# Row maxima of the attention as four narrow matmuls through the identity, and sixteen modulation units moved from GpSimd to VectorE

## The chip, the cores and the metric

The kernel runs on one core of a Trainium2 chip. The metric is the device time of one execution in microseconds; lower is better. The core has TensorE (PE in the profile; PEld is its weight load), VectorE (DVE), ScalarE (ACT), GpSimd (POOL) and SyncE (SP), which here issues the loads.

## The reference

A two-layer trunk over 512 latent tokens and 256 context tokens, width 1024. Layer 0 mixes with dense grouped attention (16 heads on 4 key heads, head size 64), layer 1 with a Conformer convolution, and each layer ends with a squared-ReLU MLP of width 4096. The parts that the change touches:

```python
def modulate(x, g, shift, scale):
    return rms_norm(x, g) * (1 + scale) + shift

# (shift, scale, gate) of both sub-layers: linear(SiLU(c)), 6 vectors of 1024 a layer
# x += gate * f(modulate(x, g, shift, scale))

def gqa_attend(q, k, v):
    p = jax.nn.softmax(gqa_scores(q, k), axis=-1)
    return jnp.einsum('bhgqk,bkhd->bqhgd', p.astype(v.dtype), v)
```

For latent tokens the keys are all 768 tokens.

## The kernel before

Activations stand transposed, features on the 128 partitions and tokens along the free axis. The products are split in high and low fp32r parts and take three passes (`passes`, L630 to L632).

**Modulation units.** Ten of the twelve vectors are computed as the program goes, in 80 units: a unit is a 128x1024 f32 tile `mraw` of the modulation weight, multiplied with the SiLU row `sbc` and summed along the free axis to one column of `mcol`. `mod_run(k)` runs the next k units; `mod_fetch` keeps two tiles loaded (tag `mraw`, two buffers), and a load is issued on SyncE when the unit before the last is done with its buffer. 64 units run on VectorE, one instruction each (L664) with its sum read out (DVE_READ_ACCUMULATOR). The first 16, those of two vectors that the output projection and the MLP need, run inside the attention loop on GpSimd: a product (L657), five halvings (L660) and a last addition (L662) into a buffer `mparts`, which VectorE reduces after the loop, before `mod_final` adds the bias.

**The attention loop.** It runs over 99 groups g; head h and key tile t are `divmod(g, 6)`. It stands in `manual_schedule` for TensorE, ScalarE and VectorE, so that these engines take their work in the order of the program. A group issues, in this order: the scores of tile t (two matmuls 128x512, L1420 and L1421) and their exponential on ScalarE; for tile 3 the split of it into high and low parts (`phl`, L1432, on VectorE); the product with v of tile g - 2 (L1439; for tile 3 the three passes); a piece of the row maxima of the next head but one or so; q's copies for later heads (L1365 and L1367); the steps of `finish` for every second head (`dn`, `rd`, `ou`, `hl`, L1469 to L1479); and at t = 2 the modulation units, two in heads 0, 4 and 8, one in each other up to head 12.

**Row maxima.** For a head, `row_max` has for each of four query tiles two matmuls 128x384 into a PSUM bank `sn` (L1377), each followed by a maximum on VectorE (L1379). `max_diag` takes the negative maximum over the pieces, with queries on the partitions (`nn`, 128x4, L1383), and multiplies it with the identity into four diagonal matrices side by side (L1385, 128x512). `max_row`, two groups later, multiplies a matrix of ones with these (L1392, 512 columns), which gives a bank with the row of 512 maxima in every partition, and ScalarE copies one partition into row 64 of `q2`, so that the second scores matmul subtracts the maximum. Three banks hold `sn`, three `mm`, two `pv`. The first two heads' maxima are made ahead of the loop, in the q projection.

Names in the rows are those of the tiles: `t` is any tile that `tmp()` gives, and the numbers behind names are of the tile's instance.

Of the kernel before, what the change touches and what calls it, by code (L numbers as in the profile page):

```python
# [344 lines left out]
def trunk(ctx: ExitStack, tc: tile.TileContext, par, cst, xT, cT, modp, modt, wqkv, wo, up, down, pw1, wtoe, pw2, out):  # L345
    nc = tc.nc
    pers = ctx.enter_context(tc.tile_pool(name="pers", bufs=1))
    wraw = ctx.enter_context(tc.tile_pool(name="wraw", bufs=2))
    whl = ctx.enter_context(tc.tile_pool(name="whl", bufs=4))
    sm = ctx.enter_context(tc.tile_pool(name="sm", bufs=4))  # L350
    tp = ctx.enter_context(tc.tile_pool(name="tp", bufs=1))

    def tmp(n=512, dt=F32):
        return tp.tile([P, n], dt, tag="t", name="t", bufs=6)
# [25 lines left out]
    ident = cst_t[:, 0:P]  # L380
    sel = pcol("sel", 0, 2)[0:4]

    ones = pers.tile([P, P], F32, name="ones")
    nc.vector.memset(ones, 1.0)
    inv_d = pers.tile([P, P], F32, name="inv_d")
    nc.vector.memset(inv_d, 1.0 / D)
    ones_r = pers.tile([P, P], F32R, name="ones_r")
    nc.scalar.copy(ones_r, ones)

    def act_set(name):  # L390
        tc.keep_in_program_order(nc.scalar.preload_act_table_set(name))
# [210 lines left out]
    fin = [None]  # L602
# [31 lines left out]
    mcol = pers.tile([P, 12, NT], F32, name="mcol")  # L634
# [3 lines left out]
    sbc = pers.tile([P, D], F32, name="sbc")  # L638

    def mod_slot(l, v):  # L640
        return l * 6 + v

    mod_raw = []
# [5 lines left out]
            nc.sync.dma_start(raw, modt[idx, b, :, i * 1024:(i + 1) * 1024])  # L649
            mod_raw.append(raw)  # L650

    def mod_unit(raw, idx, b, i, pool):
        l, v = MODV[idx]
        s = mod_slot(l, v)
        if pool is not None:
            n = 1024
            nc.gpsimd.tensor_tensor(out=raw, in0=raw, in1=sbc, op=ALU.mult)  # L657
            while n > 32:
                n //= 2
                nc.gpsimd.tensor_tensor(out=raw[:, :n], in0=raw[:, :n], in1=raw[:, n:2 * n], op=ALU.add)  # L660
            o = idx * 128 + (2 * b + i) * 16
            nc.gpsimd.tensor_tensor(out=pool[:, o:o + 16], in0=raw[:, :16], in1=raw[:, 16:32], op=ALU.add)  # L662
            return
        nc.vector.scalar_tensor_tensor(  # L664
            out=tmp(1024, mybir.dt.bfloat16), in0=raw, scalar=1.0, in1=sbc, op0=ALU.mult, op1=ALU.mult,
            accum_out=mcol[:, s, 2 * b + i:2 * b + i + 1])
        if b == 3 and i == 1:
            mod_final(l, v)

    def mod_final(l, v):  # L670
        s = mod_slot(l, v)
        mb = pcol("modb", l * 48 + v * 8, 8)
        nc.vector.tensor_tensor(out=mcol[:, s], in0=mcol[:, s], in1=mb, op=ALU.add)
        if v in (1, 4):
# [254 lines left out]
    with ExitStack() as st0:  # L929
# [83 lines left out]
        tiles, rows, w_hl, tots, msq, lrow, l_r, srow = {}, {}, {}, {}, {}, {}, {}, {}  # L1013
# [227 lines left out]
        for t_, gname in ((tk, "kg"), (tq, "qg")):  # L1241
            go = COFF[gname][0]
            for ci, cn in enumerate(("cos", "sin")):
                co = COFF[cn][0]
                for hf in range(2):
                    with tc.issue_after(tiles["pool"].ins):
                        nc.gpsimd.tensor_tensor(
                            out=t_[:, :, ci, hf * 32:(hf + 1) * 32],
                            in0=cst_t[:, co:co + 128].rearrange("p (t d) -> p t d", t=4),
                            in1=cst_t[:, go + hf * 32:go + (hf + 1) * 32].unsqueeze(1).to_broadcast([P, 4, 32]),  # L1250
                            op=ALU.mult)
        kg = cst_t[:, COFF["kg"][0]:COFF["kg"][0] + HD]

        def vview(t):
            return t.rearrange("p t (a b d) -> p t a b d", a=2, b=3)
# [123 lines left out]
                nc.vector.tensor_reduce(out=nmx[h][:, tt, b:b + 1], in_=sn[:, :384], op=ALU.max, axis=AX.X)  # L1379

        def max_diag(h):
            nm = sm.tile([P, 4], F32, tag="nn", name="nn")
            nc.vector.tensor_reduce(out=nm, in_=nmx.pop(h), op=ALU.max, axis=AX.X, negate=True)  # L1383
            dg = tmp(512, F32R)
            nc.vector.tensor_tensor(  # L1385
                out=dg.rearrange("p (t q) -> p t q", t=4), in0=ident.unsqueeze(1).to_broadcast([P, 4, P]),
                in1=nm.unsqueeze(2).to_broadcast([P, 4, P]), op=ALU.mult)
            return dg

        def max_row(h, dg):  # L1390
            mb = ms_bank()
            nc.tensor.matmul(mb, lhsT=ones_r, rhs=dg, start=True, stop=True)  # L1392
            nc.scalar.copy(qs[h][1][HD:HD + 1], mb[HD:HD + 1])

        for c in range(2):
# [89 lines left out]
        mparts = tmp(384)  # L1485
        pend = {}
        pvs = {}
        with tc.manual_schedule(engines={mybir.EngineType.PE, mybir.EngineType.Activation, mybir.EngineType.DVE}):
            for g in range(NH * NKT + 3):
                h, t = divmod(g, NKT)  # L1490
# [22 lines left out]
                while tasks.get(g):  # L1513
                    tasks[g].pop(0)()
                if t == 2 and h < NH:
                    with tc.issue_after(last_scale.ins):
                        mod_run(2 if h % 4 == 0 and h < 12 else 1 if h < 13 else 0, mparts)
                if g == NH * NKT - 12:
                    w_prefetch(1)
        with tc.issue_after(fin[0].ins):  # L1520
            for i in range(2):
                l, v = MODV[i]
                nc.vector.tensor_reduce(out=mcol[:, mod_slot(l, v)],
                                        in_=mparts[:, i * 128:(i + 1) * 128].rearrange("p (n q) -> p n q", q=16),
                                        op=ALU.add, axis=AX.X)
                mod_final(l, v)

    def proj_residual(l, v, after):
        sq = SqAcc(nc.vector)
# [298 lines left out]
```

## Time and profile before

| | |
|---|---|
| three runs | 1312.84, 1311.84, 1305.18 us (median 1311.84) |
| the profiled execution | 1310.47 us, its span 1308.7 us |
| mean granted TensorE clock | 0.977 |
| busy share | TensorE 94%, VectorE 76%, ScalarE 53%, GpSimd 19% |
| GpSimd busy | 247.1 us, of which 105.37 us from 156.27 to 285.25 us |

The attention loop begins at 147.0 us with head 0; head 1 begins at 156.27, head 12 at 285.25, head 13 at 295.18 and head 14 at 304.79. The start of a head is here the start of its first scores matmul on TensorE. The span is what the profiler recorded; the execution's own time lies 1.8 us above it.

### The profile page before, as it was taken

Reading aid. Unit: us, or ns where it says so; the run is one execution under the profiler, and the core shown is the slowest. Engines: PE = TensorE matmul, PEld = TensorE weight load, DVE = VectorE, ACT = ScalarE, POOL = GpSimd, SP = SyncE. Lnnn points to the kernel's source line nnn. Section 1 sums busy time; section 2 is a strip of 40 time slices with the busy share of each in tenths; the row PEclk is TensorE's granted clock in tenths of the full one; section 3 lists DMA queues with packets and bytes.
Section 4 is the critical chain, followed back from the end, with each engine's and each line's share of the span. In section 5 each row is a group of like instructions: output and inputs, shape, how many; then the busy total and the mean of one; then the engine's idle time right before and its main releaser. Section 6 shows DMA issues by size and latency. Waiting matters only on the chain.

```text
span 1308.7 us, 18182 instructions
## 1 busy us (share of the span) xinstructions
PE 1228.9 (94%) x6916; PEld 1037.1 (79%) x6916; DVE 1001.1 (76%) x1683; ACT 693.8 (53%) x1299; POOL 247.1 (19%) x283
## 2 busy tenths in 40 slices
PE   6789988899998999999999899896999999999998
PEld 5667655556996888888998888775998898989887
DVE  6899989978687689877785878778688766666653
ACT  7666456668245343445453386567556455455450
POOL 3444578850000000000000144323200000000000
PEclk9999999999999999999999899897999999999999
DMA  9421022213627665453534221110212132322221
GB/s 337 159 97 65 1 64 65 65 65 111 215 96 256 208 209 187 151 172 121 189 119 173 79 81 65 58 40 33 97 66 97 65 130 68 126 89 105 97 97 65
DMA packets 31623, 149.92 MB, mean 115 GB/s; under 512 B 3504, under 2 KB 3888, under 8 KB 20656
## 3 DMA queue, kind: packets, MB, share of 16 engines
q1 hardware_dynamic: 31536, 148.76, 33.2%
q8 instruction: 54, 0.88, 0.3%
q14 instruction: 33, 0.27, 0.1%
HBM read 146.65 MB, written 2.10 MB: 114 GB/s over the span
## 4 chain that ended last, share of the span: by engine, by line
PE 67%; DVE 17%; ACT 7%; issue 4%; DMA 4%; POOL 0%; SPq 0%; DVEq 0%; ACTq 0%; POOLq 0%
PE sn L760 15%; PE mm L630 8%; PE mm L632 8%; PE mm L631 8%; PE pv L631 6%; PE pv L632 6%; PE pv L630 6%; PE pv L1439 3%; ACT z L1616 2%; DVE wlo L424 2%; DVE nm L1379 2%; PE pv L1605 1%; DVE z L1581 1%; PE sn L1377 1%; DMA mraw<-in_modt_dram 1%
## 5 line engine op out<-in xcount | busy, mean ns | idle before, releaser
L419 ACT CAST whi<-raw 128x1024 fp32r<-128x1024 f32 x128 | 132.4, 1049 | 169.6 <-PE mm L631 59.4
L424 DVE TENSOR_TENSOR wlo<-raw,whi 128x1024 fp32r<-128x1024 f32 x124 | 150.5, 1221 | 51.5 <-ACT whi L419 50.0
L630 PE MATMUL mm<-hh,whi 128*128 128x256 f32 (+1 forms) x408 | 134.7, 331 | 0.0
L632 PE MATMUL mm<-hh,wlo 128*128 128x256 f32 (+1 forms) x408 | 134.6, 331 | 0.0
L631 PE MATMUL mm<-hl,whi 128*128 128x256 f32 (+1 forms) x408 | 133.5, 328 | 0.0
L630 PE MATMUL mm<-ah,whi 128*128 128x512 f32 (+1 forms) x324 | 123.8, 383 | 3.1 <-DVE x L922 3.1
L631 PE MATMUL mm<-al,whi 128*128 128x512 f32 (+1 forms) x324 | 123.6, 382 | 0.0
L632 PE MATMUL mm<-ah,wlo 128*128 128x512 f32 (+1 forms) x324 | 123.4, 381 | 0.0
L630 PE MATMUL pv<-hh,whi 128*128 128x256 f32 (+1 forms) x264 | 84.7, 321 | 10.9 <-ACT hh L1712 4.3
L455 DVE TENSOR_TENSOR wlo<-raw,whi 128x1024 fp32r<-128x1024 f32 (+1 forms) x80 | 86.7, 1086 | 9.2 <-ACT whi L447 9.0
L664 DVE SCALAR_TENSOR_TENSOR t<-mraw,sbc 128x1024 bf16<-128x1024 f32 x64 | 78.4, 1226 | 17.1 <-DMA mraw<-in_modt_dram 17.0
L447 ACT CAST whi<-raw 128x1024 fp32r<-128x1024 f32 (+1 forms) x80 | 75.2, 941 | 30.3 <-PE sn L760 13.1
L807 DVE SCALAR_TENSOR_TENSOR x<-mm,mcol,x 128x512 f32<-128x512 f32 x65 | 48.7, 749 | 54.5 <-PE mm L632 54.5
L760 PE MATMUL sn<-hl,whi 128*128 128x256 f32 x320 | 89.8, 281 | 0.0
L760 PE MATMUL sn<-hh,wlo 128*128 128x256 f32 x320 | 89.8, 281 | 0.0
L760 PE MATMUL sn<-hh,whi 128*128 128x256 f32 x320 | 89.7, 280 | 0.0
L631 PE MATMUL pv<-al,whi 128*128 128x512 f32 (+1 forms) x224 | 85.9, 384 | 3.9 <-DVE al L707 3.9
L1570 POOL MEMSET inv_h<- 128x128 f32 x1 | 0.2, 209 | 454.3 <-PE mm L632 454.3
L632 PE MATMUL pv<-ah,wlo 128*128 128x512 f32 (+1 forms) x224 | 85.9, 384 | 0.0
L630 PE MATMUL pv<-ah,whi 128*128 128x512 f32 (+1 forms) x224 | 85.7, 382 | 0.0
L631 PE MATMUL pv<-hl,whi 128*128 128x256 f32 (+1 forms) x264 | 84.1, 318 | 0.9 <-POOL hl L1713 0.9
L630 PEld LDWEIGHTS mm<-hh,whi 128*128 128x128 f32 x408 | 78.7, 193 | 7.8 <-issue 0.8
(363 smaller groups left out, 3494.3 us busy)
## 6 DMA issues: line engine op xcount, KB each, us to landing
mraw<-in_modt_dram SPq DMA_DIRECT2D x80, 512.0 KB, 4.4
raw<-in_up_dram SPq DMA_DIRECT2D x32, 1024.0 KB, 4.9
raw<-in_down_dram SPq DMA_DIRECT2D x32, 1024.0 KB, 5.0
raw<-in_pw_dram SPq DMA_DIRECT2D x12, 1024.0 KB, 4.9
mraw<-in_modp_dram SPq DMA_DIRECT2D x10, 512.0 KB, 8.7
raw<-in_wqkv_dram SPq DMA_DIRECT2D x5, 1024.0 KB, 5.0
x<-in_xT_dram SPq DMA_DIRECT2D x16, 256.0 KB, 6.2
raw<-in_wo_dram SPq DMA_DIRECT2D x4, 1024.0 KB, 4.9
```

Source lines behind the costliest of these rows:

```text
L419: nc.scalar.copy(hi, raw[:, i * 1024:(i + 1) * 1024])
L424: eng.tensor_tensor(out=lo, in0=raw[:, i * 1024:(i + 1) * 1024], in1=hi.bitcast(F32), op=ALU.subtract)
L447: nc.scalar.copy(hi[:, :n], raw[:, o:o + n])
L455: nc.vector.tensor_tensor(out=lo[:, :n], in0=raw[:, o:o + n], in1=hi[:, :n].bitcast(F32), op=ALU.subtract)
L630: nc.tensor.matmul(acc, lhsT=ahi, rhs=bhi, start=first, stop=False)
L631: nc.tensor.matmul(acc, lhsT=ahi, rhs=blo, start=False, stop=False)
L632: nc.tensor.matmul(acc, lhsT=alo, rhs=bhi, start=False, stop=last)
L664: nc.vector.scalar_tensor_tensor(out=tmp(1024, mybir.dt.bfloat16), in0=raw, scalar=1.0, in1=sbc, op0=ALU.mult, op1=ALU.mult, accum_out=mco ...
L760: nc.tensor.matmul(acc, lhsT=a, rhs=b, start=first and k == 0 and i == 0, stop=k == 3 and i == 2, skip_group_check=not first)
L807: nc.vector.scalar_tensor_tensor(out=x[j], in0=acc, scalar=col(l, 5, j), in1=x[j], op0=ALU.mult, op1=ALU.add)
L1379: nc.vector.tensor_reduce(out=nmx[h][:, tt, b:b + 1], in_=sn[:, :384], op=ALU.max, axis=AX.X)
L1439: nc.tensor.matmul(pv, lhsT=vt[:, f, i:i + P], rhs=p_, start=t == 0, stop=t == NKT - 1)
```

## The change

`max_diag` leaves the diagonals out and returns the four columns of negative maxima, now fp32r. `max_row` makes four matmuls of 128 columns, each with one of these columns, repeated 128 times, as weights and the identity `ident_r` as what moves; each fills a quarter of the same bank. `ident_r` is made once by GpSimd in the q projection, and the fp32r matrix of ones and its copy are gone. The 16 units of the loop run on VectorE as the other 64 do; `mparts`, its two reduces and the GpSimd instructions are gone, and the constraint that held the units back until the last scaling of q is gone too.

```diff
@@ setup
-    ones_r = pers.tile([P, P], F32R, name="ones_r")
-    nc.scalar.copy(ones_r, ones)
+    ident_r = pers.tile([P, P], F32R, name="ident_r")
@@ mod_unit
-        if pool is not None:
-            n = 1024
-            nc.gpsimd.tensor_tensor(out=raw, in0=raw, in1=sbc, op=ALU.mult)
-            while n > 32:
-                n //= 2
-                nc.gpsimd.tensor_tensor(out=raw[:, :n], in0=raw[:, :n], in1=raw[:, n:2 * n], op=ALU.add)
...
-            return
         nc.vector.scalar_tensor_tensor(
             out=tmp(1024, mybir.dt.bfloat16), in0=raw, scalar=1.0, in1=sbc, op0=ALU.mult, op1=ALU.mult,
             accum_out=mcol[:, s, 2 * b + i:2 * b + i + 1])
@@ q projection
+        with tc.issue_after(tiles["pool"].ins):
+            nc.gpsimd.tensor_copy(ident_r, ident)
@@ max_diag
-            nm = sm.tile([P, 4], F32, tag="nn", name="nn")
+            nm = sm.tile([P, 4], F32R, tag="nn", name="nn")
             nc.vector.tensor_reduce(out=nm, in_=nmx.pop(h), op=ALU.max, axis=AX.X, negate=True)
-            dg = tmp(512, F32R)
-            nc.vector.tensor_tensor(
-                out=dg.rearrange("p (t q) -> p t q", t=4), in0=ident.unsqueeze(1).to_broadcast([P, 4, P]),
-                in1=nm.unsqueeze(2).to_broadcast([P, 4, P]), op=ALU.mult)
-            return dg
+            return nm
@@ max_row
-            nc.tensor.matmul(mb, lhsT=ones_r, rhs=dg, start=True, stop=True)
+            for tt in range(4):
+                nc.tensor.matmul(mb[:, tt * P:(tt + 1) * P], lhsT=nm[:, tt:tt + 1].to_broadcast([P, P]), rhs=ident_r,
+                                 start=True, stop=True)
@@ the loop
                 if t == 2 and h < NH:
-                    with tc.issue_after(last_scale.ins):
-                        mod_run(2 if h % 4 == 0 and h < 12 else 1 if h < 13 else 0, mparts)
+                    mod_run(2 if h % 4 == 0 and h < 12 else 1 if h < 13 else 0)
...
-        with tc.issue_after(fin[0].ins):
-            for i in range(2):
-                l, v = MODV[i]
-                nc.vector.tensor_reduce(out=mcol[:, mod_slot(l, v)], ...
-                mod_final(l, v)
```

The order of instructions on VectorE at the end of the q projection and in head 0, before; L555 to L558 are steps of the last q tile's rstd, and `phl` is head 0's split.

```order
L1294 TENSOR_TENSOR qnat<-t 128x8x32
L1365 CAST q_1600<-qt 64x512
L555 TENSOR_TENSOR s_1559<-s_1557 128x8
L1367 TENSOR_TENSOR q_1599<-qt,q_1600 64x512
L556 SCALAR_TENSOR_TENSOR s_1559<-s_1559,s_1552 128x8
L558 SCALAR_TENSOR_TENSOR s_1562<-s_1559,s_1557 128x8
L1432 TENSOR_TENSOR phl<-pp,phl 128x512
```

The same place after:

```order
L1286 TENSOR_TENSOR qnat<-t 128x8x32
L1357 CAST q_1601<-qt 64x512
L1359 TENSOR_TENSOR q_1600<-qt,q_1601 64x512
L554 TENSOR_TENSOR s_1561<-s_1559 128x8
L654 SCALAR_TENSOR_TENSOR t,mcol<-mraw,sbc 128x1024
L555 SCALAR_TENSOR_TENSOR s_1561<-s_1561,s_1554 128x8
L654 SCALAR_TENSOR_TENSOR t,mcol<-mraw,sbc 128x1024
L557 SCALAR_TENSOR_TENSOR s_1564<-s_1561,s_1559 128x8
L1422 TENSOR_TENSOR phl<-pp,phl 128x512
```

Two units (L654 is L664 of before) now stand among the steps of the rstd.

VectorE in head 12 and the beginning of head 13, before:

```order
L1383 TENSOR_REDUCE nn<-nm 128x4
L1385 TENSOR_TENSOR t<-cst_t,nn 128x512
L1365 CAST q_2800<-qt 64x512
L1367 TENSOR_TENSOR q_2799<-qt,q_2800 64x512
L1432 TENSOR_TENSOR phl<-pp,phl 128x512
L1379 TENSOR_REDUCE nm<-sn 128x1 x2
L1469 TENSOR_TENSOR dn<-dn,rd 128x512
L1470 SCALAR_TENSOR_TENSOR rd<-dn,rd 128x512
```

The same place after:

```order
L1375 TENSOR_REDUCE nn<-nm 128x4
L1357 CAST q_2736<-qt 64x512
L1359 TENSOR_TENSOR q_2735<-qt,q_2736 64x512
L654 SCALAR_TENSOR_TENSOR t,mcol<-mraw,sbc 128x1024 x2
L663 TENSOR_TENSOR mcol<-mcol,par_t 128x8
L1422 TENSOR_TENSOR phl<-pp,phl 128x512
L1371 TENSOR_REDUCE nm<-sn 128x1 x2
L1459 TENSOR_TENSOR dn<-dn,rd 128x512
L654 SCALAR_TENSOR_TENSOR t,mcol<-mraw,sbc 128x1024
L1460 SCALAR_TENSOR_TENSOR rd<-dn,rd 128x512
```

The diagonal is gone, and besides the loop's own unit of head 12 there are units of the output projection: its four (L664) stood in heads 14 and 15 before, and in heads 12 and 13 now, two of them further down. SyncE's loads of `mraw` for them stand ahead of the two loads of the output weights.

TensorE in the same head, before:

```order
L1439 MATMUL pv<-pp,vt 128x512
L1377 MATMUL sn<-k_3_897,q_2873 128x384 x2
L1392 MATMUL sn<-t,ones_r 128x512
L1420 MATMUL mm<-q_2676,k_3_897 128x512
L1421 MATMUL mm<-q_2677,k_3_901 128x512
```

And after:

```order
L1429 MATMUL pv<-pp,vt 128x512
L1369 MATMUL sn<-k_3_897,q_2808 128x384 x2
L1381 MATMUL sn<-ident_r,nn 128x128 x4
L1410 MATMUL mm<-q_2618,k_3_897 128x512
L1411 MATMUL mm<-q_2619,k_3_901 128x512
```

One matmul has become four at the same place.

## Rows read from the trace of the kernel before

**Rows 1.** The page's chain of work that ended last, by engine.

```profile
PE 67%; DVE 17%; ACT 7%; issue 4%; DMA 4%; POOL 0%; SPq 0%; DVEq 0%; ACTq 0%; POOLq 0%
```

**Rows 2.** Stretches: us, busy PE PEld DVE ACT POOL, granted clock, DMA, GB/s.

```profile
156.27:285.25 128.98, 113.88 (x395) 71.67 (x395) 114.13 (x163) 79.10 (x141) 105.37 (x112) 0.97 0.19 62
285.25:295.18 9.93, 9.93 (x40) 6.66 (x39) 6.90 (x14) 6.96 (x13) 0.00 (x0) 1.00 0.15 54
295.18:304.79 9.61, 9.61 (x36) 6.23 (x35) 8.62 (x17) 7.56 (x14) 0.00 (x0) 1.00 0.00 0
304.79:331.00 26.21, 25.05 (x113) 17.11 (x113) 19.68 (x31) 18.90 (x31) 0.00 (x0) 1.00 0.49 161
270.00:278.00 8.00, 6.40 (x20) 3.89 (x18) 7.97 (x8) 3.71 (x7) 7.84 (x5) 0.79 0.03 13
147.00:156.27 9.27, 8.00 (x32) 5.12 (x31) 8.65 (x20) 6.87 (x16) 4.04 (x4) 1.00 0.00 1
```

**Rows 3.** TensorE's waits in heads 1 to 11: us, times, longest.

```profile
PE sn L1377 <- DVE nm L1379: 4.6, 3, 1.9
PE sn L1392 <- DVE t L1385: 3.8, 3, 1.5
```

**Rows 4.** VectorE's groups in heads 1 to 11: busy us, mean ns, idle before.

```profile
L1379 DVE TENSOR_REDUCE nm<-sn 128x1 f32<-128x384 f32 x88 | 44.7, 549 | 10.3 <-PE sn L1377 9.9
L1385 DVE TENSOR_TENSOR t<-cst_t,nn 128x512 fp32r<-128x512 f32 x11 | 13.2, 1197 | 0.4
L1432 DVE TENSOR_TENSOR phl<-pp,phl 128x512 fp32r<-128x512 f32 x11 | 12.4, 1132 | 3.0 <-ACT phl L1427 2.9
```

**Rows 5.** The same groups in heads 12 and 13.

```profile
L1379 DVE TENSOR_REDUCE nm<-sn 128x1 f32<-128x384 f32 x16 | 8.2, 552 | 1.8 <-PE sn L1377 1.7
L1385 DVE TENSOR_TENSOR t<-cst_t,nn 128x512 fp32r<-128x512 f32 x2 | 1.4, 692 | 0.1
L1432 DVE TENSOR_TENSOR phl<-pp,phl 128x512 fp32r<-128x512 f32 x2 | 1.4, 689 | 1.6 <-ACT phl L1427 1.6
L1473 DVE SCALAR_TENSOR_TENSOR ou<-ou,rd 128x512 f32<-128x512 f32 x1 | 0.7, 681 | 0.0
```

**Rows 6.** Timeline near 227 us: start, length.

```profile
226.60 2.35 POOL L657 TENSOR_TENSOR mraw<-mraw,sbc 128x1024 f32<-128x1024 f32 x1
226.91 2.59 DVE L1473 SCALAR_TENSOR_TENSOR ou<-ou,rd 128x512 f32<-128x512 f32 x1
```

**Rows 7.** Tile mraw from 100 to 330 us: who waited; loads.

```profile
  POOL mraw L657: 20.2, 7
DMA to landing us min/median/max: 3.5/4.2/5.3
```

**Rows 8.** Timeline of TensorE: one row's product, scores, one weighing.

```profile
227.33 1.02 PE L1439 MATMUL pv<-pp,vt 128*128 128x512 f32 x2
293.38 0.39 PE L1392 MATMUL sn<-t,ones_r 128*128 128x512 f32 x1
293.61 0.40 PE L1420 MATMUL mm<-q,k 128*128 128x512 f32 x1
```

**Rows 9.** Narrow matmuls of the convolution: a run; all (ns min/median/max).

```profile
775.52 1.50 PE L1605 MATMUL pv<-u,tz 128*128 128x128 f32 x12
L1605 PE MATMUL pv<-u,tz x402: 269/275/377, 771.4 to 892.9; 128*128 128x128 f32 x134
```

**Rows 10.** Timeline of VectorE: a unit and its read-out.

```profile
311.55 1.22 DVE L664 SCALAR_TENSOR_TENSOR t<-mraw,sbc 128x1024 bf16<-128x1024 f32 x1
312.69 0.08 DVE L664 DVE_READ_ACCUMULATOR t<-mraw,sbc 128x1 f32 x1
```

**Rows 11.** Timeline of VectorE: phl in head 12 and in head 13.

```profile
293.22 0.69 DVE L1432 TENSOR_TENSOR phl<-pp,phl 128x512 fp32r<-128x512 f32 x1 [1.59 <-ACT phl L1427]
302.27 0.69 DVE L1432 TENSOR_TENSOR phl<-pp,phl 128x512 fp32r<-128x512 f32 x1
```

**Rows 12.** Timeline of GpSimd in head 0.

```profile
154.66 1.43 POOL L1297 TENSOR_TENSOR qnat<-qnat,s 128x512 f32<-128x512 f32 x1 [1.88 <-DVE s L558]
```

More of the change, by code (lines that the diff above doesn't have):

```diff
@@ L650, in mod_fetch, with mod_unit @@
             mod_raw.append(raw)
-    def mod_unit(raw, idx, b, i, pool):
+    def mod_unit(raw, idx, b, i):
         l, v = MODV[idx]
         s = mod_slot(l, v)
-        if pool is not None:
-            n = 1024
-            nc.gpsimd.tensor_tensor(out=raw, in0=raw, in1=sbc, op=ALU.mult)
-            while n > 32:
-                n //= 2
-                nc.gpsimd.tensor_tensor(out=raw[:, :n], in0=raw[:, :n], in1=raw[:, n:2 * n], op=ALU.add)
-            o = idx * 128 + (2 * b + i) * 16
-            nc.gpsimd.tensor_tensor(out=pool[:, o:o + 16], in0=raw[:, :16], in1=raw[:, 16:32], op=ALU.add)
-            return
         nc.vector.scalar_tensor_tensor(
@@ L680, in trunk, with mod_run @@
     mod_pos = [0]
-    def mod_run(k, pool=None):
+    def mod_run(k):
         for _ in range(k):
@@ L688, in mod_run @@
                 mod_pos[0] += 1
-                mod_unit(mod_raw.pop(0), *u, pool)
+                mod_unit(mod_raw.pop(0), *u)
                 mod_fetch()
@@ L1381, in max_diag, with max_row @@
         def max_diag(h):
-            nm = sm.tile([P, 4], F32, tag="nn", name="nn")
+            nm = sm.tile([P, 4], F32R, tag="nn", name="nn")
             nc.vector.tensor_reduce(out=nm, in_=nmx.pop(h), op=ALU.max, axis=AX.X, negate=True)
-            dg = tmp(512, F32R)
-            nc.vector.tensor_tensor(
-                out=dg.rearrange("p (t q) -> p t q", t=4), in0=ident.unsqueeze(1).to_broadcast([P, 4, P]),
-                in1=nm.unsqueeze(2).to_broadcast([P, 4, P]), op=ALU.mult)
-            return dg
-        def max_row(h, dg):
+            return nm
+        def max_row(h, nm):
             mb = ms_bank()
-            nc.tensor.matmul(mb, lhsT=ones_r, rhs=dg, start=True, stop=True)
+            for tt in range(4):
+                nc.tensor.matmul(mb[:, tt * P:(tt + 1) * P], lhsT=nm[:, tt:tt + 1].to_broadcast([P, P]), rhs=ident_r,
+                                 start=True, stop=True)
             nc.scalar.copy(qs[h][1][HD:HD + 1], mb[HD:HD + 1])
@@ L1483, in finish @@
                     later(g if last else g + 1 + k, fn)
-        mparts = tmp(384)
         pend = {}
@@ L1515, in trunk @@
                 if t == 2 and h < NH:
-                    with tc.issue_after(last_scale.ins):
-                        mod_run(2 if h % 4 == 0 and h < 12 else 1 if h < 13 else 0, mparts)
+                    mod_run(2 if h % 4 == 0 and h < 12 else 1 if h < 13 else 0)
                 if g == NH * NKT - 12:
                     w_prefetch(1)
-        with tc.issue_after(fin[0].ins):
-            for i in range(2):
-                l, v = MODV[i]
-                nc.vector.tensor_reduce(out=mcol[:, mod_slot(l, v)],
-                                        in_=mparts[:, i * 128:(i + 1) * 128].rearrange("p (n q) -> p n q", q=16),
-                                        op=ALU.add, axis=AX.X)
-                mod_final(l, v)
     def proj_residual(l, v, after):
```

## The prediction

> **What bounds the kernel now.** I read the chain of waits first, to see which engine sets the end over the whole run, then the table of stretches, because the change touches one stage only, then the groups of VectorE instructions in two stretches of that stage, and last single instructions on the timeline. The chain [rows 1] says TensorE for two thirds; that is an average, and in the attention loop it is wrong. The loop's head pace shows it [rows 2]. Heads 1 to 11, in which GpSimd works on the modulation units, take 128.98 us, 11.73 each; VectorE is busy 114.13 of them and TensorE 113.88, so TensorE is idle 15.1. Heads 12 and 13, with the same work and GpSimd silent, take 9.93 and 9.61; TensorE is busy all through, and VectorE only 6.90 and 8.62. So without GpSimd the bound is TensorE, at some 9.8 us a head, and with GpSimd it is VectorE: the largest waits of TensorE in heads 1 to 11 are on VectorE's row maxima and on the diagonal [rows 3]. In the worst eight microseconds VectorE is busy 7.97 of 8.00, TensorE 6.40, and the granted clock falls to 0.79, that is, part of the time at 1.2 instead of 2.4 GHz [rows 2].
>
> Why is VectorE slow there? The same instructions last longer: the diagonal 1197 ns against 692, the phl difference 1132 against 689; but the maximum that reads PSUM takes 549 against 552 [rows 4, 5]. The timeline has one case: VectorE's ou, 0.68 in heads 12 and 13 [rows 5], runs 226.91 to 229.50 and GpSimd's multiply 226.60 to 228.95 [rows 6]. So VectorE's SBUF instructions end only after the GpSimd instruction they overlap. The Trainium skill, page "SBUF — State Buffer", section "Who interferes with whom", gives a rule for this: VectorE's second pair of SBUF ports is shared with GpSimd and held by one of the two for a whole instruction, and a tensor_reduce never contends. The 1197 against 692 ns and the 549 against 552 agree with it.
>
> **The change part by part.** The sum is made against the profiled execution's 1310.47 us (span 1308.7), which is 1.4 under the median of the three runs.
>
> A. The units leave GpSimd. Each of the 16 units of the loop is seven GpSimd instructions, a product, five halvings and the last addition, 112 in all and 105.37 us [rows 2]. They go, and with them the slowing of heads 1 to 11. If these eleven heads take the pace of heads 12 and 13 (five even at 9.93, six odd at 9.61; an odd head's finish serves two), they take 49.65 + 57.66 = 107.31, so 128.98 - 107.31 = **-21.7**. This is the whole gain.
>
> B. Row maxima. Per head, one matmul of 512 columns becomes four of 128. In the trace a 512-column one is followed by the next after 0.23 us [rows 8]. A narrow record of 128 columns advances every (1.50 - 0.28) / 11 = 0.11 us, the 0.28 being the length of one alone [rows 9]. Those records are of plain f32, which leaves two records per matmul (L1439 likewise, one matmul that the trace has as x2); L1392 leaves one [rows 8], and so I take four times 0.112 less 0.23 = +0.22 a head, times 16 heads: **+3.5**, since TensorE is then the bound. From below it is 0, if the narrow ones hide in their neighbours; from above, with two passes each, 4 x 0.224 - 0.23 = +0.67, times 16 = +10.7. No row shows weights that are one column read 128 times, so a slower load lies in the upper end. The diagonal's VectorE instruction goes (0.69 clean); the -max itself stays. The copy of the row on ScalarE is unchanged, and it has four groups of the loop until its head's scores need it. GpSimd's one copy into ident_r comes in a stretch of the q projection in which GpSimd isn't waited for, and costs nothing; if that cover is gone, it is an eighth of the multiply's 2.35 [rows 6] by elements, an estimate of 0.3. The ones_r copy on ScalarE goes, where that engine waits for its first data: nothing.
>
> C. The loop's 16 units on VectorE. One unit is 1.22 + 0.08 = 1.30 us [rows 10] against 0.69 for the diagonal it replaces: +0.61 of VectorE a head. In an even head VectorE waits 1.59 us in front of phl [rows 11], where the diagonal and the unit stand just before, so 0.69 + 1.59 covers 1.30: nothing. In an odd head VectorE is busy 8.62 of 9.61, so 0.61 more fits into 0.99 idle, but the diagonal is followed at once by phl, which TensorE's three passes (L630 to L632) wait for: I take a third of the excess, +0.2, times 6 heads = +1.2. Heads 4 and 8 have two units, 2.60 against a cover of 2.28: 0.32 if all of it serves, 1.30 if none is left for the second; I take +0.6 each = +1.2. Together **+2.4**. The lower end is 0, if one-unit heads hide all and the scores of tile 3 have slack; the upper 6 x 0.61 + 2 x 1.30 = 6.3.
>
> D. Units of the output projection. The order shows what the diff doesn't: four units that stood in heads 14 and 15 now stand in heads 12 and 13, where VectorE's queue goes in program order. Demand there: 15.5 busy (6.90 + 8.62) less two diagonals 1.4 plus five units 6.5, one of them of part C, = 20.6 in a stretch of 19.54; the waits of 1.6 and 1.8 that are now idle can't all be filled. Behind a unit stand reduces that free the sn banks, and TensorE waits for these. From 20.6 + 3.4 - 19.5 = 4.5 as the largest by VectorE alone, plus up to 0.7 for a landing, an estimate (a landing takes 3.5 to 5.3 us after its issue [rows 7], and two units in a row take both buffers), and 20.6 - 19.5 = 1.1 as the smallest, I take **+3.5**.
>
> E. Heads 14 and 15 lose these four units, 5.2 us of VectorE. TensorE is idle 26.21 - 25.05 = 1.16 in the stretch from head 14 to 331 us [rows 2], so no more than that can come back: **-0.8** (0 to -1.2).
>
> F. Head 0 and the step ahead of it: two units (2.6) now stand among the small steps of the last rstd of q, and two diagonals (1.38) go: **+1.2**. The lower end is -0.5: the units lie in VectorE's waits, and a third of the diagonals' 1.38 comes back. The upper is +2.9: each unit is also held for one of GpSimd's products of qnat, 2 x 1.43 [rows 12]. What is queued behind: the last products of qnat on GpSimd wait for that rstd, and q of head 1 for them; the first head takes 9.27 with TensorE busy 8.00 [rows 2]. The Trainium skill speaks against the change in this one place: by the same section a VectorE instruction with two SBUF inputs, such as the unit, contends with a GpSimd instruction that reads SBUF, as those products do. By it F would be at its upper end and the sum 1300.2; without it, as taken, 1298.5. No row shows a unit beside them yet.
>
> Sum: -21.7 + 3.5 + 2.4 + 3.5 - 0.8 + 1.2 = -11.9, so 1310.47 - 11.9 = **1298.5 us**. The rest of the program (conv, both MLPs) has the same instructions in the same order, and I give it 0.
>
> **The rivals.** (1) The narrow matmuls cost two passes each: B is 10.7 instead of 3.5, +7.2, so 1305.7. For it: the only 128-column matmuls in the trace are of this sort; against: the 512-column one is recorded once. (2) VectorE stays the bound. Its excess of 0.61 a head, eleven times, and two second units of 1.30 make 9.3 in place of C's 2.4: 1305.4. For it: before the change VectorE was the bound over just this stretch, and its order is fixed, so a unit delays a reduce that TensorE waits for. Against: VectorE's idle time in heads 12 and 13 is 4.0 of 19.54. (3) Slower: VectorE waits for landings. GpSimd waited 20.2 us in 7 waits for the mraw loads [rows 7], 2.9 each. On GpSimd that cost nothing by itself; on VectorE, which works in order, each holds the reduces, the finish and the split behind it. Sixteen such waits are 46 us, 1310.5 - 11.9 + 46 = 1345; the kernel gets slower from 11.9 / 16 = 0.75 us a unit. Against: two buffers, loads on a queue that does little else here (62 GB/s [rows 2]), and some 10 us between units against a landing of 4.2. (4) It doesn't do what it says: VectorE's long instructions are long for another reason than GpSimd's, and then only B to F count: the eleven heads stay bound by VectorE, lose 13.2 of diagonals (11 x 1.197) and gain 13 units, 16.9, and D to F add 3.9: 1310.5 + 3.7 + 3.9 = 1318. Against it stands the stop of the slowing in head 12 with GpSimd's last instruction.
>
> **How the numbers follow.** Forecast 0.57; rival 1 0.18, since the form that it speaks of is not in the trace; rival 2 0.14; rival 4 0.06; rival 3 0.05. The forecast's own bounds downward: A could give 2 more (odd heads at the pace of even ones, 6 x 0.32), B 3.5, C 2.4, D 2.4, E 0.4, F 1.7, together 12.4; upward C 3.9, D 1.7, E 0.8, F 1.7, together 8.1. They won't all come at once: three quarters of each gives 1289.2 and 1304.6, and rivals 1 and 2 lie at 1305.7 and 1305.4, with a way to go beyond. Range **1289 to 1308**. A measurement of this kernel can tell about 1%, 13.1 us, from no change; the forecast's 11.9 is just short of that, but its bounds reach half as far again down as up. So 0.6 of its 0.57, which is 0.34, and 0.06 of rivals 1 and 2, where the rest falls out well, are faster by over 1%: 0.40. Slower is rival 3, 0.05. Within 1%: 0.55.
>
> **What would show it.** In the profile after: VectorE's phl and ou in heads 1 to 11 at 0.69 and 0.68 (A, against rival 4); the head pace there 9.8 to 10.2, and the granted clock at 1.00 throughout the loop; the stride of the four narrow matmuls 0.11 or 0.22 (B, rival 1); TensorE's waits on nm in heads 4, 8, 12 and 13 (C, D) and whether they are in all heads (rival 2); waits of the unit's line on its load (rival 3). I would be wrong if TensorE's waits on VectorE don't shrink, or if the pace without GpSimd isn't set by TensorE.

## The result and the profile after

The changed kernel takes 1291.39 us (median of 1289.31 to 1294.13, 4 runs) against 1308.62 before (1305.18 to 1312.84, 4 runs), a ratio of 0.986 with a 95% interval of 0.9836 to 0.9884. That is 17.2 us less; the forecast was 1298.5, 11.9 less, with a range of 1289 to 1308. The profiled executions are 1310.47 and 1290.80, 19.7 apart. The result lies in the range, near its lower end; the forecast gave 0.40 to "faster by over 1%", which is what the interval shows, and 0.55 to "within 1%". (In the line numbers of after, L654 is the unit, L1371 and L1375 the maxima, L1381 the narrow matmuls, L1410 and L1411 the scores, L1422 phl.)

The stretches after, which answer to [rows 2]: head 0, heads 1 to 11, head 12, head 13, the rest to 314 us, and eight microseconds within head 11.

```profile
148.70:157.40 8.70, 7.74 (x31) 5.00 (x30) 7.75 (x17) 6.00 (x13) 2.72 (x3) 1.00 0.20 56
157.40:265.94 108.54, 108.54 (x428) 73.65 (x428) 92.01 (x179) 79.20 (x141) 0.00 (x0) 1.00 0.20 67
265.94:276.04 10.10, 10.10 (x43) 6.90 (x42) 8.65 (x18) 7.19 (x13) 0.00 (x0) 1.00 0.23 77
276.04:287.89 11.85, 10.27 (x38) 6.30 (x38) 11.36 (x22) 7.38 (x14) 0.00 (x0) 1.00 0.42 139
287.89:314.10 26.21, 24.98 (x116) 17.54 (x116) 14.68 (x21) 18.88 (x31) 0.00 (x0) 1.00 0.27 95
259.00:267.00 8.00, 8.00 (x34) 5.50 (x32) 7.15 (x15) 5.57 (x11) 0.00 (x0) 1.00 0.18 66
```

Heads 1 to 11 went from 128.98 to 108.54, and TensorE is busy in all of it, at a granted clock of 1.00, that is 2.4 GHz throughout. VectorE is busy 22.1 us less there, although it does 13 units more. Of the 20.4, 15.1 is what TensorE was idle before; the rest is TensorE's own busy time, 113.88 before at a granted clock of 0.97, with fewer matmuls (395 against 428), and how much of that the clock made is not separated. VectorE's groups in heads 1 to 11 (columns as in [rows 4]):

```profile
L1371 DVE TENSOR_REDUCE nm<-sn 128x1 f32<-128x384 f32 x88 | 44.8, 550 | 11.1 <-PE sn L1369 10.8
L654 DVE SCALAR_TENSOR_TENSOR t<-mraw,sbc 128x1024 bf16<-128x1024 f32 x13 | 15.7, 1220 | 0.2
L1422 DVE TENSOR_TENSOR phl<-pp,phl 128x512 fp32r<-128x512 f32 x11 | 7.6, 688 | 3.5 <-ACT phl L1417 3.5
L1463 DVE SCALAR_TENSOR_TENSOR ou<-ou,rd 128x512 f32<-128x512 f32 x5 | 3.4, 680 | 0.0
```

phl is at 688 ns (1132 before, [rows 4]), ou at 680, the maximum from PSUM unchanged at 550. The unit waits for nothing: 0.2 us of idle time before 13 of them. TensorE's list of waits in heads 1 to 11 is empty after; before it held 4.6 and 3.8 us as its largest [rows 3]. The chain that ended last has less of VectorE in it (17% before, [rows 1]):

```profile
PE 76%; DVE 11%; ACT 6%; issue 4%; DMA 2%; POOL 0%; SPq 0%; DVEq 0%; ACTq 0%; POOLq 0%
```

Where it lost is head 13: 11.85 us, TensorE busy 10.27, VectorE 11.36. VectorE's timeline there (start, length; in brackets the wait and who ended it):

```profile
276.61 1.23 DVE L654 SCALAR_TENSOR_TENSOR t<-mraw,sbc 128x1024 bf16<-128x1024 f32 x1 [0.31 <-DMA mraw<-in_modt_dram]
277.76 0.08 DVE L654 DVE_READ_ACCUMULATOR t<-mraw,sbc 128x1 f32 x1
277.76 0.69 DVE L1460 SCALAR_TENSOR_TENSOR rd<-dn,rd 128x512 f32<-128x512 f32 x1
278.37 1.01 DVE L1371 TENSOR_REDUCE nm<-sn 128x1 f32<-128x384 f32 x2
```

And TensorE's:

```profile
278.97 0.44 PE L1369 MATMUL sn<-k,q 128*128 128x384 f32 x1 [1.25 <-DVE nm L1371]
```

A unit that came between dn and rd, and waited 0.31 for its load besides, stands in front of the maximum that frees a bank, and TensorE waits 1.25 for that bank. A second wait comes at the end of the head, behind the last of the four units, which stands in front of phl:

```profile
286.97 0.50 PE L630 MATMUL pv<-phl,vh 128*128 128x512 f32 x1 [0.33 <-DVE phl L1422]
```

The whole difference of the profiled runs, by the starts of the same TensorE instructions: up to the first product of the q projection +0.5; from there to the end of head 0 +0.6; heads 1 to 11 -20.4; heads 12 and 13 +2.4; head 14 -0.3; the output projection with the beginning of the MLP -1.9; all the rest -0.3. Together -19.4. The -1.9 is the landing of one load. ScalarE's cast of the first up weights waited 2.91 us for it before; after:

```profile
335.49 2.00 ACT L418 CAST whi<-raw 128x1024 fp32r<-128x1024 f32 x2 [0.99 <-DMA raw<-in_up_dram]
```

The run gp_write2 below has the same instructions in this stretch as late4, which waited 1.14, and yet it has the long wait again:

```profile
337.14 2.00 ACT L418 CAST whi<-raw 128x1024 fp32r<-128x1024 f32 x2 [2.98 <-DMA raw<-in_up_dram]
```

Over all the profiles this wait lies between 0.8 and 3.0 us, so this part is not put down to the change. Nor is the +0.5: the first product of the q projection starts at 92.0 us after, and between 91.5 and 95.0 in the twelve other profiles. The change's own part is some 18 us.

### The profile page after: what moved, and what is told of

It reads as the page before. It is cut to its first block, busy times and chain, and to the rows that moved or that the text cites. A ratio compares the mean times of both kernels' runs of the same rounds, so it can differ in the third digit from the quotient of the medians.

```text
span 1289.0 us, 18175 instructions
## 1 busy us (share of the span) xinstructions
PE 1228.3 (95%) x6964; PEld 1043.4 (81%) x6964; DVE 977.4 (76%) x1697; ACT 692.6 (54%) x1297; POOL 141.8 (11%) x172
## 4 chain that ended last, share of the span: by engine, by line
PE 76%; DVE 11%; ACT 6%; issue 4%; DMA 2%; POOL 0%; SPq 0%; DVEq 0%; ACTq 0%; POOLq 0%
PE sn L750 15%; PE mm L629 9%; PE mm L631 9%; PE mm L630 9%; PE pv L630 6%; PE pv L629 6%; PE pv L631 6%; PE pv L1429 4%; ACT z L1597 3%; PE sn L1369 2%; PE mm L1411 1%; PE mm L1410 1%; PE pv L1586 1%; DVE wlo L423 1%; PE mm L1105 1%
## 5 line engine op out<-in xcount | busy, mean ns | idle before, releaser
L654 DVE SCALAR_TENSOR_TENSOR t<-mraw,sbc 128x1024 bf16<-128x1024 f32 x80 | 97.4, 1221 | 15.7 <-DMA mraw<-in_modt_dram 15.4
L454 DVE TENSOR_TENSOR wlo<-raw,whi 128x1024 fp32r<-128x1024 f32 (+1 forms) x80 | 86.7, 1086 | 11.6 <-ACT whi L446 11.5
L631 PEld LDWEIGHTS mm<-hh,wlo 128*128 128x128 f32 x408 | 78.5, 193 | 7.6 <-issue 0.5
```

The source lines that it names most:

```text
L454: nc.vector.tensor_tensor(out=lo[:, :n], in0=raw[:, o:o + n], in1=hi[:, :n].bitcast(F32), op=ALU.subtract)
L631: nc.tensor.matmul(acc, lhsT=alo, rhs=bhi, start=False, stop=last)
L654: nc.vector.scalar_tensor_tensor(out=tmp(1024, mybir.dt.bfloat16), in0=raw, scalar=1.0, in1=sbc, op0=ALU.mult, op1=ALU.mult, accum_out=mco ...
```

## The experiments

Theory 1: instructions of GpSimd that read SBUF hold VectorE's SBUF instructions; without them TensorE sets the pace of the loop and the units lie in VectorE's idle time. Theory 2: the gain is that VectorE, the bound, lost its diagonals. Theory 3: VectorE was slow for another reason that the change removed by the way. Stretches below are always heads 1 to 11, and heads 12 and 13 where a second row stands. Behind the time of each run stand its ratio to the kernel before, which was measured again beside it (medians of 1308.7 to 1311.6 us), and the 95% interval of this ratio.

**Either part alone.** units_only moves the units and keeps the diagonals; rows_only has the narrow matmuls and leaves the units on GpSimd.

```diff
 # units_only, against after
+            dg = tmp(512, F32R)
+            nc.vector.tensor_tensor(out=dg..., in0=ident..., in1=nm..., op=ALU.mult)
...
-            for tt in range(4):
-                nc.tensor.matmul(mb[:, tt * P:(tt + 1) * P], lhsT=nm[:, tt:tt + 1].to_broadcast([P, P]), rhs=ident_r, ...)
+            nc.tensor.matmul(mb, lhsT=ones_r, rhs=dg, start=True, stop=True)
 # rows_only, against before: the reverse, and mod_run(ticks[0]) of the output
 # projection stands under tc.issue_after(the negative maximum of head 15)
```

> The units run on VectorE as in the change, but the diagonals, the matrix of ones and the 512-column product stay. Theory 1 (GpSimd's instructions hold VectorE's, and without them TensorE sets the pace): heads 1 to 11 take 107 to 109 us, the diagonal is back to 0.69 us, heads 12 and 13 about 19.6 since the projection's units stay in heads 14 and 15 here; 1288 to 1293 us. Theory 2 (the gain is VectorE's 13.2 us of diagonals that went, VectorE being the bound): heads 1 to 11 stay at 120 us or more, 1300 to 1305 us.

> The row maxima go through the identity as in the change, but the units stay on GpSimd as before (the projection's units are held in heads 14 and 15, where they stood). Theory 1: the remaining instructions of VectorE stay long (phl 1.0 to 1.2 us in heads 1 to 11); the 13.2 us of diagonals go from the engine that is the bound there, but part of what GpSimd holds shifts to its neighbours: heads 1 to 11 at 118 to 125 us, 1299 to 1307 us. Theory 2: all 13.2 come off, 1293 to 1298 us, and together with the run that moves the units alone the two gains add up to that of the change.

units_only: 1295.8 us, 0.9876 (0.9852 to 0.9901). rows_only: 1299.53, 0.9915 (0.989 to 0.994). The two stretches of units_only:

```profile
163.12:274.52 111.40, 110.39 (x395) 70.71 (x395) 99.05 (x190) 79.10 (x141) 0.00 (x0) 0.99 0.19 60
274.52:294.06 19.54, 19.54 (x74) 12.87 (x73) 16.92 (x33) 14.53 (x26) 0.00 (x0) 1.00 0.13 47
```

Those of rows_only:

```profile
158.91:280.34 121.43, 112.59 (x428) 72.67 (x428) 102.06 (x152) 79.30 (x141) 98.31 (x105) 1.00 0.19 61
280.34:300.08 19.74, 19.74 (x79) 13.45 (x79) 14.32 (x28) 14.57 (x26) 2.35 (x8) 1.00 0.16 53
```

One of VectorE's groups in units_only, the diagonal, is back at 692 ns:

```profile
L1376 DVE TENSOR_TENSOR t<-cst_t,nn 128x512 fp32r<-128x512 f32 x11 | 7.6, 692 | 0.4
```

One in rows_only, phl, is still slow:

```profile
L1436 DVE TENSOR_TENSOR phl<-pp,phl 128x512 fp32r<-128x512 f32 x11 | 12.9, 1172 | 6.8 <-ACT phl L1431 6.7
```

Moving the units alone takes 17.6 us off heads 1 to 11, the row maxima alone 7.6; together they would give 25.1, and the change gave 20.4. They don't add up, because both work on the same excess of VectorE and TensorE's pace ends it. That speaks against theory 2. units_only came 2 to 4 us over what theory 1 gave it: heads 1 to 11 took 111.4 where 107 to 109 was expected (heads 1, 4 and 8 are at 10.5, heads 6, 7, 10 and 11 at 9.9), and head 0 took 12.74 against 9.27 before, with a wait of TensorE of 2.6 us on phl behind diagonals and two units. With the diagonals kept, the units are not quite free, so the two parts need each other there.

**GpSimd put back to work.** Four kernels are built on late4 (below), the change with the projection's units held in heads 14 and 15; it is the base that they are compared with. After each of the loop's units GpSimd gets some 6 to 7 us of work whose result nobody uses: on the unit's own tile (gp_copy the old product and halvings, gp_write fills), or on a buffer of its own (gp_read2 products, gp_write2 fills). The last two also hold the loop's units back until the last scaling of q, as the kernel before did; since both do, they can be compared with each other.

```diff
 # gp_copy                                # gp_write
+ nc.gpsimd.tensor_tensor(out=raw, in0=raw, in1=sbc, op=ALU.mult)
+ while n > 16: ... add of the halves     + for n in range(6): nc.gpsimd.memset(raw, 0.5)
 # gp_read2 and gp_write2: first nc.gpsimd.tensor_copy(gsc[:, :1], raw[:, :1]), then
+ 5x nc.gpsimd.tensor_tensor(out=gsc, in0=sbc[:, :512], in1=sbc[:, 512:], op=ALU.mult)
+ 13x nc.gpsimd.memset(gsc, 0.5)
 # and in both mod_run of the loop stands under tc.issue_after(last_scale.ins)
```

> The kernel with the projection's units held late, and after each of the loop's units on VectorE GpSimd works through the same tile once more, with the product and six halvings as before, its result unused. Theory 1 (GpSimd's instructions that read SBUF hold VectorE's): phl goes back to 1.0 to 1.3 us, the PSUM maxima stay at 0.55, heads 1 to 11 take 118 to 126 us instead of 108.57, and the unit itself gets longer than 1.22. Theory 3 (VectorE was slow for another reason, such as the shape of the queue or the tile buffers, which the change has removed): heads 1 to 11 stay at 108 to 110.

> The same place on GpSimd, but six fills of the whole tile in place of the product and the halvings, so that GpSimd is as busy and only writes. The rule of the Trainium skill (page SBUF — State Buffer, section Who interferes with whom) has it that an instruction of VectorE with two SBUF inputs contends with a GpSimd instruction that reads SBUF, not with one that only writes it: phl stays at 0.69, only the cast of q may get longer, heads 1 to 11 stay at 108.5 to 109.5. Rival: any GpSimd instruction holds VectorE's: phl at 0.9 or more, heads 1 to 11 at 112 us or more.

> The kernel with the projection's units held late; after each of the loop's units GpSimd copies one column of the tile and then makes five products of the two halves of sbc into a buffer of its own, some 7 us that read SBUF and leave the modulation tile's buffer free, so that no load comes later. Theory 1: phl at 1.0 us or more, heads 1 to 11 at 113 to 122 us, and VectorE's waits for loads under 3 us. Theory 3 (what cost time in the other two runs with GpSimd at work was the held buffer): heads 1 to 11 at 108.5 to 110.

> The same with thirteen fills of that buffer in place of the five products, some 6 to 7 us that only write. If the loss of 16.5 us with fills of the modulation tile was the held buffer (VectorE waited 11.6 us for loads there): heads 1 to 11 at 108.5 to 109.5, phl at 0.69. If fills hold VectorE as well: 111 or more.

gp_copy: 1332.19, 1.0179 (1.0154 to 1.0203). gp_write: 1305.0, 0.9967 (0.9949 to 0.9986). gp_read2: 1322.97, 1.0106 (1.0057 to 1.0154). gp_write2: 1289.95, 0.985 (0.9801 to 0.99). The stretch of gp_read2:

```profile
158.87:302.26 143.39, 122.17 (x429) 77.30 (x429) 129.33 (x180) 79.37 (x141) 128.97 (x96) 0.93 0.17 56
```

Three of its VectorE groups there:

```profile
L1383 DVE TENSOR_REDUCE nm<-sn 128x1 f32<-128x384 f32 x89 | 45.5, 549 | 12.8 <-PE sn L1381 12.1
L1434 DVE TENSOR_TENSOR phl<-pp,phl 128x512 fp32r<-128x512 f32 x11 | 16.0, 1459 | 0.0
L1369 DVE CAST q<-qt 64x512 fp32r<-64x512 f32 x11 | 9.0, 818 | 0.1
```

The stretch of gp_write2:

```profile
159.02:268.14 109.12, 109.12 (x428) 73.43 (x428) 94.09 (x179) 79.26 (x141) 98.08 (x191) 1.00 0.21 68
```

And the same three groups there:

```profile
L1383 DVE TENSOR_REDUCE nm<-sn 128x1 f32<-128x384 f32 x88 | 44.8, 551 | 10.3 <-PE sn L1381 10.0
L1434 DVE TENSOR_TENSOR phl<-pp,phl 128x512 fp32r<-128x512 f32 x11 | 7.6, 689 | 3.0 <-ACT phl L1429 3.0
L1369 DVE CAST q<-qt 64x512 fp32r<-64x512 f32 x11 | 6.7, 606 | 0.2
```

VectorE's and TensorE's orders and data are the same in both. With reads GpSimd's 129 us cost 34.8 over late4's 108.57 (21.2 of them TensorE's idle time, the rest its longer busy time at a granted clock of 0.93), and phl lasts 1459 ns; with fills GpSimd's 98 us cost 0.55, phl stays at 689, and only the cast is longer (421 in late4). The maximum from PSUM is untouched in both. gp_read2 lost more than the 113 to 122 that was expected: GpSimd is busy 129 of 143 us there, so that few of VectorE's instructions find it silent. This settles theory 1 against theory 3. The Trainium skill (page "SBUF — State Buffer", section "Who interferes with whom") says that two SBUF inputs contend with GpSimd's reads and not with its writes, and that a cast can contend too. The trace agrees: phl goes from 689 to 1459 ns beside reads only, the cast from 421 to 606 beside fills. GpSimd's product itself lasts 1.53 us here, so phl's excess of 0.77 is half of one.

gp_copy and gp_write took more than expected, because they hold the modulation tile's buffer for 6 us or more, and the load after next comes late. Their stretches:

```profile
159.84:304.42 144.58, 126.20 (x429) 81.96 (x429) 109.42 (x179) 79.34 (x141) 90.39 (x98) 0.89 0.16 51
158.86:283.94 125.08, 116.23 (x428) 76.92 (x428) 93.58 (x179) 79.28 (x141) 79.59 (x86) 0.95 0.19 59
```

In gp_copy phl lasts 1438 ns and the unit 1407, so both losses are in it. In gp_write phl is at 687, and of VectorE's instructions only the cast is longer (542); gp_write2, where it is longer still, lost 0.55. What is lost is the waits for loads:

```profile
L659 DVE SCALAR_TENSOR_TENSOR t<-mraw,sbc 128x1024 bf16<-128x1024 f32 x13 | 15.9, 1223 | 11.7 <-DMA mraw<-in_modt_dram 11.6
```

Five waits of VectorE, 11.6 us, cost 16.5. This is the mechanism of the prediction's rival 3 with its price: VectorE's order is fixed, and its waits for loads cost the loop more than their length. The change is spared it because a unit on VectorE frees its buffer at once.

**How free the units are.** Both are built on late4 too. no_loop_units leaves the loop's 16 units out, with what they compute (the columns are set to zero, and the count of units starts at 16); units_twice runs each twice.

```diff
 # no_loop_units                          # units_twice, behind each unit of the loop
-  mod_run(2 if h % 4 == 0 ...)           + nc.vector.scalar_tensor_tensor(out=tmp(...), in0=raw, ...,
+  pass                                   +     in1=sbc, ..., accum_out=gacc)
```

> The kernel with the projection's units held late, but without the loop's 16 units: the MLP's shift and the attention's gate are left at their biases, nothing else is left out. Theory 1 (with GpSimd silent TensorE sets the pace and the units are hidden behind it): heads 1 to 11 within 0.5 us of the 108.57 with units, VectorE busy some 17 us less there. Theory of the forecast's term C: the units are on the path in part, and these heads take 1.5 to 2.5 us less, 106 to 107.

> The kernel with the projection's units held late, and each of the loop's units runs twice on VectorE, the second time into a column that nothing reads: 1.30 us more a unit, 13 of them in heads 1 to 11, 16.9 us. VectorE was busy 92.0 of 108.5 there. Theory 1 (units are free until VectorE's idle time is used up, and TensorE waits then): odd-numbered and even-numbered heads part ways; those with one unit take 0.2 to 0.6 more, those with two 1.5 to 2.5 more, heads 1 to 11 at 111 to 117. Rival (a unit costs its full length from the first on): the same 1.30 each, 108.57 + 16.9 = 125; and if even twice is free, 109.

no_loop_units: 1286.99, 0.9846 (0.9821 to 0.987). units_twice: 1303.02, 0.9952 (0.9925 to 0.9978). The stretch of late4, for comparison:

```profile
159.32:267.89 108.57, 108.57 (x428) 73.63 (x428) 92.06 (x179) 79.22 (x141) 0.00 (x0) 1.00 0.21 67
```

That of no_loop_units:

```profile
156.35:264.82 108.47, 108.47 (x428) 73.80 (x428) 77.62 (x152) 79.18 (x141) 0.00 (x0) 1.00 0.00 1
```

And that of units_twice:

```profile
162.14:281.01 118.87, 114.08 (x428) 75.26 (x428) 106.54 (x205) 79.22 (x141) 0.00 (x0) 0.97 0.17 56
```

Without the units VectorE has 14.4 us less and the heads take 0.10 less: the 13 units of heads 1 to 11 are free. units_twice lost 10.3, a little over the 2 to 8 that theory 1 gave it and well under the 16.9 of its rival. The even heads with two passes of a unit are free as well (heads 2, 6 and 10 take 10.07 to 10.09, as in late4); the odd ones 3, 7, 9 and 11 pay 0.5 to 0.8, heads 1 and 5, each behind a head with four, pay 2.1 and 1.0, and heads 4 and 8, with four, 2.0 and 2.7. So after the change VectorE has room for one more unit in an even head and, where no head with four stands before it, for about half a one in an odd head.

**The narrow matmuls, doubled.** rows_twice is late4 with each narrow matmul made twice.

```diff
-            for tt in range(4):
+            for tt in (0, 1, 2, 3, 0, 1, 2, 3):
```

> The kernel with the projection's units held late, and each of the four narrow matmuls of a row of maxima twice, eight in place of four. Term B's working: four more of 0.112 us, +0.45 a head where TensorE is the bound, 4.9 us in heads 1 to 11 (113.5) and 0.9 in heads 12 and 13 (20.6). Rival (heads 12 and 13 took only 0.21 us more with narrow matmuls than with wide ones, so much of it is absorbed in TensorE's stalls): +0.1 to 0.25 a head, 109.7 to 111.3.

rows_twice: 1297.67, 0.9911 (0.9886 to 0.9936). Its stretches:

```profile
160.84:273.91 113.07, 113.07 (x472) 79.09 (x472) 92.34 (x179) 79.37 (x141) 0.00 (x0) 1.00 0.20 66
273.91:294.50 20.59, 20.59 (x87) 14.42 (x87) 15.72 (x31) 14.60 (x26) 0.00 (x0) 1.00 0.08 27
```

One place on TensorE's timeline in rows_twice (start, length):

```profile
281.26 0.91 PE L1374 MATMUL sn<-k,q 128*128 128x384 f32 x2
282.01 1.00 PE L1386 MATMUL sn<-ident_r,nn 128*128 128x128 f32 x8
282.85 0.45 PE L1415 MATMUL mm<-q,k 128*128 128x512 f32 x1
```

The same place in late4:

```profile
284.92 0.91 PE L1374 MATMUL sn<-k,q 128*128 128x384 f32 x2
285.66 0.56 PE L1386 MATMUL sn<-ident_r,nn 128*128 128x128 f32 x4
286.06 0.45 PE L1415 MATMUL mm<-q,k 128*128 128x512 f32 x1
286.34 0.40 PE L1416 MATMUL mm<-q,k 65*128 65x512 f32 x1
```

Four take 0.40 to the next matmul, eight 0.84, so 0.11 each, with the column repeated as weights and with one record each. Four more cost 0.41 a head, 4.5 in heads 1 to 11: term B's price was right. A head with four narrow ones, though, is only 0.1 longer than one with the wide one (19.74 in late4 against 19.54 in units_only for heads 12 and 13). Four narrow ones and the next scores matmul take 0.40 + 0.28 = 0.68 where the wide one and its next take 0.23 + 0.24, +0.21 a head. Half of it is taken up at the turn from head 12 to head 13. The last `sn` matmul of head 12 and the first two scores of head 13 take 0.24, 0.33 and 0.34 to the next one in units_only, and 0.17, 0.23 and 0.28 in late4, 0.23 less. TensorE's weight load for the second of these scores waits there for the row of maxima that ScalarE copies; in units_only:

```profile
284.77 0.19 PEld L1412 LDWEIGHTS mm<-q,k 65*128 65x128 f32 x1 [0.32 <-ACT q L1384]
```

In late4, where TensorE comes to this place later:

```profile
278.13 0.19 PEld L1416 LDWEIGHTS mm<-q,k 65*128 65x128 f32 x1 [0.16 <-ACT q L1388]
```

In rows_twice this wait is gone, and the four more cost their full price.

**A version that puts the units elsewhere.** late4 holds the output projection's four units behind the last head's negative maxima; late4_shift also moves head 0's two units to heads 2 and 6.

```diff
+            held[0] = nc.vector.tensor_reduce(out=nm, in_=nmx.pop(h), op=ALU.max, axis=AX.X, negate=True)
...
+            with tc.issue_after(held[0].ins):
                 mod_run(ticks[0])
 # late4_shift besides:
-                    mod_run(2 if h % 4 == 0 and h < 12 else 1 if h < 13 else 0)
+                    mod_run(0 if h == 0 else 2 if h % 2 == 0 and h < 9 else 1 if h < 13 else 0)
```

> The change, with the four units of the output projection held behind the last head's negative maxima, so that they stand in heads 14 and 15 as before. Theory 1 (units in heads 12 and 13 made VectorE the bound there): heads 12 and 13 take 19.7 to 20.0 us instead of 21.95, heads 14 and 15 up to 1 us more; 0.9 to 2.2 us faster than the change. Rival: the four units cost the same wherever they stand, and the sum of heads 12 to 15 stays within 0.3 us.

> As the run that holds the projection's units, and head 0's two units go to heads 2 and 6 as second ones, so none stands among the steps of the last rstd of q. Theory 1 (two units ahead of head 0 delayed its start by 1.7 us; a second unit in an even head is hidden): the first scores of head 0 start 1.2 to 1.7 us earlier, heads 2 and 6 stay at 10.1; 1 to 2 us faster than the run without the shift. Rival: a second unit isn't hidden, heads 2 and 6 take 0.6 to 1.3 more each, and nothing is left of it.

late4: 1289.21, 0.9835 (0.9804 to 0.9866). late4_shift: 1288.6, 0.9823 (0.9796 to 0.9849). Heads 12 and 13 of late4:

```profile
267.89:287.63 19.74, 19.74 (x79) 13.46 (x79) 15.72 (x31) 14.57 (x26) 0.00 (x0) 1.00 0.10 35
```

They take 19.74 instead of 21.95, head 14 takes 8.93 in both, and head 15 up to the output projection 10.55 and 10.62, so 2.2 us of the change's price is the pull-up of the four units alone, as theory 1 had it. late4_shift's head 0 takes 7.77 instead of 8.70 and its heads 1 to 11 108.79 instead of 108.57; a second unit in heads 2 and 6 costs 0.02 and 0.14. But the start of head 0, counted from the first product of the q projection, is 57.15 us there and 56.71 in late4, so head 0's units had not delayed it; that expectation fell, and the whole is 0.6 us shorter than late4 and not 1 to 2. Against the 55.51 of before, the start comes later with the row maxima alone (57.17 in rows_only) and not with the units alone (55.49 in units_only). Both versions are shorter than the change in the stages named; their intervals overlap that of the change, so that they beat it is shown in these stages and not in the whole time.

## Why the prediction was right, and where its sizes were off

The main step, **A**, held in mechanism and size. The pace of heads 12 and 13 before was taken over to heads 1 to 11, 107.31; without any units and with narrow matmuls they took 108.47, and 11 times the 0.1 that a head is longer by the narrow ones makes up the 1.16 between. That leaves -21.7 for A, as forecast; no run has the old row maxima with neither units nor GpSimd, so A and B are told apart by this estimate. What all the other steps were forecast to give back, 9.8, was 4.0 or so.

**B** was forecast at +3.5 and was about +1.4: +1.2 in heads 1 to 11, +0.2 in heads 12 and 13. The price of a narrow matmul, 0.11, was right, and rival 1 (two passes) fell. The step that failed is "since TensorE is then the bound": TensorE is busy all through heads 12 and 13 by the rows, but at the turn between them its scores wait for the row of maxima, and half of the 0.22 went into that wait.

**C** was forecast at +2.4 and was 0.1. The step that failed is "I take a third of the excess, +0.2, times 6 heads" and the 0.6 in heads 4 and 8: a unit of 1.30 in place of a diagonal is covered in odd heads as well, and a second one in heads 4 and 8. With the diagonal kept it is not: in units_only heads 4 and 8 took 10.53, where head 12 took 9.93 before, and in head 11 the first two passes of the weighing, which need phl, take 0.42 and 0.34 to the next matmul, where late4 has 0.23 and 0.23. units_twice shows where the cover ends, and rival 2, with VectorE as the bound, lies beyond that point.

**D** was forecast at +3.5 and was +2.2, all of it in head 13, in the way that was described: a unit in front of the maximum that frees a bank, 0.31 of it a landing, and another in front of phl.

**E** was forecast at -0.8; head 14 gave 0.3, but not by the units that left it. It takes 8.93 in late4 and rows_only as well, where these units stand in heads 14 and 15, and 9.22 before and 9.23 in units_only. What left it is the diagonal, behind which phl came late; before:

```profile
313.44 0.51 PE L631 MATMUL pv<-phl,vh 128*128 128x512 f32 x1 [0.24 <-DVE phl L1432]
```

From head 15 until late in the output projection there is nothing that stands out from the runs (41.1 to 42.8 us in all profiles, 42.2 in both of these). So the step that failed in E is that the four units cost anything in heads 14 and 15.

**F** was forecast at +1.2 and was +0.6. Its upper end did not come up: the units end at 155.74, and GpSimd's product of qnat, which waits for the rstd behind them, starts at 155.90, so the two never ran side by side in this profile. The rule of the Trainium skill (page "SBUF — State Buffer", section "Who interferes with whom") that spoke against the change in this place found nothing to act on.

Sum: -21.7 + 1.4 + 0.1 + 2.2 - 0.3 + 0.6 = -17.7, which goes with the 17.2 between the medians. The forecast was short by the uncertain terms B, C, D and F, which all came out lower than they were set, in part for reasons of their own.

Two readings in the prediction are not right, though the forecast does not hang on them. Under the bounds downward, "odd heads at the pace of even ones" would make A smaller, since an odd head is the shorter one; even heads at the pace of odd ones would give 5 x 0.32 = 1.6 more, which moves the lower end of the range by 0.3. And "only after the GpSimd instruction they overlap" is more than the trace has: of the 11 diagonals in heads 1 to 11 before, four last 691 to 694 ns, and by the timeline not all of these stand clear of GpSimd's instructions; the other seven last 801 to 2805. The 1197 is a mean of both kinds.

Rival 3 did not come up in the change, but its mechanism is real (gp_write); what prevents it is that the buffer is free when the unit's one instruction ends. Rival 4 fell with phl at 688 ns and with gp_read2.

## What to carry to other kernels

Where an engine's instructions of one shape have two lengths in one trace, look for what else runs beside the long ones; the stretch in which it is silent gives the pace after the change directly, here to 1.2 us in 108.5. A row of waits on VectorE doesn't say that VectorE has too much work: here it did 13 units more and was busy 22 us less. Costs of added instructions are to be looked for where the receiving engine has no idle time in front of a releaser (head 13), not spread over all places; and what a removed instruction had held up belongs in the same sum.

## What the runs showed that was not expected

VectorE's waits for loads in gp_write cost this loop 1.4 times their length (11.6 us of waits, 16.5 us). TensorE is idle 8.9 of these 16.5; in the rest its 428 matmuls are busy 116.23 us instead of late4's 108.57, at a granted clock of 0.95. GpSimd reading beside VectorE made heads 1 to 11 as long as 143 us, longer than before the change (128.98), although GpSimd's busy time is higher by less than a quarter (105 to 129 us); VectorE has the units there besides, at 1988 ns each instead of 1220. Between the runs built on late4, with the same instructions up to there, the start of the q projection differs by up to 3 us, and one landing in the MLP by 2, so that effects under 3 us have to be read by stage.
